# Output and down projections token-major, part of down in a 7-product block form, rope keys padded to full rows

## The chip, the cores and the metric

The kernel runs on one core of one Trainium2 chip. The metric is the time of the device in microseconds for one execution; the table below gives the runs and one execution taken with the hardware profiler. Engines are named as the profile names them: PE is TensorE's matmul, PEld its weight load, DVE is VectorE, ACT is ScalarE, POOL is GpSimd, SP issues DMAs.

## What is computed

One decoder layer for 256 tokens of width 2048, in fp32: three mixers side by side (a pool mixer, latent attention with 8 heads, attention to a memory of 256 tokens), an output projection with a residual, and a gated feed-forward of width 5632 with a short causal convolution, with a residual.

```python
h = rms_norm(x, g_mix[l])
z = h @ w_in[l]
z_pool, z_q, z_kv, z_kr, z_mq = jnp.split(z, IN_SPLITS, axis=-1)
...
x = x + jnp.concatenate([y_pool, y_mla, y_mem], axis=-1) @ w_o[l]
x = x + conv_glu_ffn(rms_norm(x, g_ffn[l]), w_gate[l], w_up[l], conv_w[l], conv_b[l], w_down[l])
...
return (jax.nn.silu(gc) * (h @ w_up)) @ w_down
...
k = jnp.concatenate([k_nope, k_r], axis=-1)
```

The third line from below closes the feed-forward; `gc` is the convolution of `h @ w_gate` along the tokens. The last line is from the latent attention: a head's key is 128 columns of its own and a rope key of 64 that all heads share.

## The kernel before

Every fp32 operand of a large product is split into a high part, rounded to the type that TensorE takes in one pass, and a low part, the rest. A product is then three: high x high, high x low, low x high. For weights `split_w` does it: ScalarE casts the high part (L90), VectorE subtracts it from the weights for the low part (L91), 1024 columns at a time. The parts lie in rings of three buffers (`wh`, `wl`), the raw weights in a ring of three buffers of 1 MB (`wr`), loaded through SP's queue by `load_w`.

There are two forms of product. `gemm_t` is feature-major: a weight tile of 128 x 128 is stationary, the activations of all 256 tokens move, with their high parts in columns 0 to 255 and their low parts in 256 to 511. The high weights take one matmul of 512 columns (L104), the low ones one of 256 (L107); the two halves of the result are added by VectorE. `gemm_n` is token-major: an activation tile (128 features x 128 tokens) is stationary and the weights move, 512 columns at a time, in three matmuls (L121 to L123) into one PSUM bank.

The order in time: keys and values of the memory (token-major), memory queries and rope key (token-major), latents and pool input (feature-major), queries and keys up (token-major), then for each of 8 heads `mla(h)` beside one `out_half(0, ...)` of the output projection, then the rest of the output projection (`out_half(1, ...)`), gate and up (44 feature tiles of 128), and down (16 output tiles, each over 44 tiles of the feed-forward). Instructions are placed by a scheduler, which moves a ready one ahead of one that waits; each engine then runs its own in the order in which they were placed.

In `mla` the scores of a head have a product over 128 rows (L577), one over the 64 rows of the rope part (L578), whose tiles hold two heads, one in rows 0 to 63 and one in 64 to 127, and a product in bf16 that adds the mask (L580); each fp32 product here is two instructions. The softmax follows; the probabilities are turned by TensorE, multiplied with the values, and split into `cat`.

The output projection adds into `xT`, which holds x feature-major. From it `h2`, the split input of the feed-forward, is made tile by tile, and the squares for the norm are summed over features (L603 to L616). The norm's factor `r1` is multiplied onto gate and up behind their products (L628). Down is feature-major, too; the result is added to `xT` (L655, L656) and leaves in 16 DMAs of 128 KB.

PSUM is two pools of four banks each: `psm` for the large products, `psa` for the others. `big` is one space of SBUF that holds the parts of the memory, then the queries, keys and values, then `h2`.

Of the kernel before, what the change touches and what calls it, by code (L numbers as in the profile page):

```python
# [18 lines left out]
P = 128  # L19
# [18 lines left out]
HS = 1024  # L38

# [11 lines left out]
# per-token tables: cos | sin (each NT x 32), rope gains of q | k (64 each), pool edge factors (4 x 16)  # L51
# [5 lines left out]
def layer(ctx, tc, xT_d, memT_d, vec_d, tab_d, w_z_d, w_mqkr_d, w_q_d, w_kv_d, w_mem_d, w_pool_d, w_o_d,  # L57
# [26 lines left out]
    def split_w(raw, o, n, cut=HS):  # L84
        """high and low parts of raw[:, o:o + n]"""
# [24 lines left out]
    def gemm_n(pss, hi, lo, act, k0, first, last):  # L110
        """pss[tt][j] (+)= act[:, k0:, tile tt].T @ W[:, :, span j]; tokens on partitions. hi/lo: [P, k, n]"""
# [13 lines left out]
    def split_act(dst, src, scale=None):  # L125
        """dst[:, :T], dst[:, T:] = high and low parts of src (times a per-partition scale)."""
# [16 lines left out]
    xT = const.tile([P, KD, T], F32, name="xT")  # L143
# [8 lines left out]
    # the tensor engine's clock is raised, and the activation tables are loaded, while the first loads are on their way  # L152
# [13 lines left out]
    mp = mix.enter_context(tc.tile_pool(name="mix", bufs=1))  # L166

# [14 lines left out]
    class SumSq:  # L182
        """sum over tiles and partitions of squares, per token"""
# [31 lines left out]
    def to_features(dst, src, tt, n, scale=None, eng=None):  # L215
        """dst[:, i, tile tt] = src[:, i * 128:].T (times a per-partition scale), i < n <= 4"""
# [116 lines left out]
    rsqrt_(rxb[:], ps[:, 0:T], 1.0 / D)  # L333

# [26 lines left out]
    def softmax_pv(ps, spans, f, v_of, dst):  # L361
        """ps: scores of each query tile at spans, keys in tiles of P; dst gets the parts of the output's transpose"""
# [12 lines left out]
        # turned: for each key tile, the query tiles that see it  # L375
# [25 lines left out]
    def half_add(dst, ps):  # L401
        """dst = ps[:, :T] + ps[:, T:]"""
# [23 lines left out]
    # scale of the normalised latents, per token: s = rx * (rx^2 mean(z^2) + eps)^-0.5  # L426
# [41 lines left out]
    qkv = big.tile([P, 32, T], F32, tag="act", name="qkv")  # L468
    qnT, knT, qrT, krT = qkv[:, 0:8], qkv[:, 8:16], qkv[:, 16:20], qkv[:, 20:24]
# [5 lines left out]
    def rotate(dst, src, s, tt, nh):  # L475
        """dst = rotated src [P, nh, 64] with the gained tables of side s"""
# [32 lines left out]
    # keys are scaled by f_k = ((s_kv^2 |kn|^2 + rx^2 |kr|^2) / QK + eps)^-0.5 and turned  # L509
# [43 lines left out]
    # f_q = s_q (s_q^2 mean + eps)^-0.5 / sqrt(QK), applied as the softmax scale  # L553
# [11 lines left out]
    for tt in range(NT):  # L565
# [3 lines left out]
        to_features(krT, t, tt, 4, None, "v")  # L569

# [1 line left out]
    def mla(h):  # L572
        ps = ps_aux()
        b = ROPE * (h % 2)
# [8 lines left out]
    def out_half(i, m):  # L583
        """x (+)= the part i of the output projection, for the pair of feature tiles m, m + 1"""
        raw = load_w(w_o_d[i][m // 2], STG)
        for j in range(2):
            ps = ps_main()
            if i == 0:
                gemm_t(ps, raw, j * HS, lambda k: cat[:, k, :] if k < 4 else catm[:, k - 4, :], range(8))
            else:  # L590
                gemm_t(ps, raw, j * HS, lambda k: cat[:, k, :], range(4, 12))
# [147 lines left out]
```

## Time and profile before

| | us |
|---|---|
| three runs, lowest, median, highest | 1044.50, 1044.92, 1044.95 |
| profiled execution, span from its first to its last instruction | 1043.6 |
| TensorE busy in it | 1034.8 |
| VectorE busy | 708.8 |
| ScalarE busy | 542.5 |

The span of the profiled execution leaves out what lies around it; it stands 1.3 us below the median of the runs. A matmul's record reaches from its start to a modelled end that lies past the start of the next, since matmuls are pipelined: the spacing of two starts is what one costs, and not the length of its record. The granted clock of TensorE is at full speed, 2.4 GHz, all through.

### The profile page before, as it was taken

The numbers are of one execution on the slowest core, as the hardware profiler recorded it, in microseconds if no ns is written. First come the engines' busy times: TensorE is split into PE (matmuls) and PEld (weight loads), VectorE is DVE, ScalarE is ACT, GpSimd is POOL, SyncE is SP. The second block draws the span as 40 slices with busy tenths as digits, with TensorE's granted clock in tenths as the row PEclk, the third lists the DMA queues.
The fourth block names the chain that finished last, engine by engine and source line by source line (L and its number), as shares of the span: only waits on it lengthen the run. The fifth ranks groups of instructions, "written<-read, shape, count | busy, mean of one in ns | idle before, by whom it ended". The sixth has DMA issues, their size and how long they took to land.

```text
span 1043.6 us, 14921 instructions
## 1 busy us (share of the span) xinstructions
PE 1034.8 (99%) x5852; PEld 897.2 (86%) x5852; DVE 708.8 (68%) x1141; ACT 542.5 (52%) x828; POOL 1.5 (0%) x10
## 2 busy tenths in 40 slices
PE   8999999999999999999999999999999999999998
PEld 6798888778888888888888888888888888888887
DVE  6967689766887777777777777777776554454453
ACT  7847666544666555555455455455454343333342
POOL 0000000000000000000000000000000000000000
PEclk9999999999999999999999999999999999999999
DMA  8555444333555555545555455555555665665661
GB/s 334 206 185 197 159 162 172 121 122 121 184 180 202 179 185 202 180 184 202 180 184 202 181 183 202 182 183 200 184 181 180 202 194 185 211 196 181 223 197 46
DMA packets 31030, 191.83 MB, mean 184 GB/s; under 512 B 3440, under 2 KB 6000, under 8 KB 10864
## 3 DMA queue, kind: packets, MB, share of 16 engines
q1 hardware_dynamic: 30672, 190.49, 52.7%
q8 instruction: 46, 0.75, 0.3%
q10 hardware_dynamic: 288, 0.38, 0.1%
q14 instruction: 24, 0.20, 0.0%
HBM read 188.77 MB, written 2.10 MB: 183 GB/s over the span
## 4 chain that ended last, share of the span: by engine, by line
PE 98%; DMA 1%; ACT 0%; DVE 0%; SPq 0%; issue 0%
PE psm L104 56%; PE psm L107 29%; PE psm L123 3%; PE psm L121 3%; PE psm L122 3%; PE psa L578 1%; PE psa L219 1%; DMA wr<-in_w_mem 1%; PE psa L385 1%; PE psa L577 1%; PE psa L380 1%; PE psa L393 0%; PE psa L386 0%; PE psa L580 0%; DVE wl L91 0%; ACT wh L90 0%
## 5 line engine op out<-in xcount | busy, mean ns | idle before, releaser
L91 DVE TENSOR_TENSOR wl<-wr,wh 128x1024 fp32r<-128x1024 f32 (+2 forms) x368 | 431.6, 1174 | 270.6 <-ACT wh L90 237.1
L90 ACT CAST wh<-wr 128x1024 fp32r<-128x1024 f32 (+2 forms) x368 | 371.2, 1009 | 438.3 <-PE psm L104 350.4
L104 PE MATMUL psm<-h,wh 128*128 128x512 f32 x1408 | 352.7, 392 | 0.0
L104 PEld LDWEIGHTS psm<-h,wh 128*128 128x128 f32 x1408 | 253.3, 189 | 45.5 <-DVE h L132 0.3
L107 PEld LDWEIGHTS psm<-h,wl 128*128 128x128 f32 x1408 | 192.1, 190 | 13.7
L107 PE MATMUL psm<-h,wl 128*128 128x256 f32 x1408 | 196.5, 282 | 0.0
L104 PE MATMUL psm<-aT,wh 128*128 128x512 f32 x704 | 177.9, 393 | 0.0
L104 PEld LDWEIGHTS psm<-aT,wh 128*128 128x128 f32 x704 | 125.9, 189 | 22.2
L107 PEld LDWEIGHTS psm<-aT,wl 128*128 128x128 f32 x704 | 97.0, 190 | 7.7
L107 PE MATMUL psm<-aT,wl 128*128 128x256 f32 x704 | 99.3, 282 | 0.0
L104 PE MATMUL psm<-cat,wh 128*128 128x512 f32 x192 | 52.0, 398 | 0.0
L642 DVE SCALAR_TENSOR_TENSOR gc<-g,vec,gc 128x255 f32<-128x255 f32 x88 | 42.2, 480 | 1.5
L104 PE MATMUL psm<-xg,wh 128*128 128x512 f32 x160 | 43.0, 401 | 0.0
L104 PEld LDWEIGHTS psm<-cat,wh 128*128 128x128 f32 x192 | 33.5, 189 | 4.9
L104 PEld LDWEIGHTS psm<-xg,wh 128*128 128x128 f32 x160 | 28.7, 189 | 4.9
L107 PEld LDWEIGHTS psm<-cat,wl 128*128 128x128 f32 x192 | 27.3, 190 | 2.6
L121 PE MATMUL psm<-wh,mg 128*128 128x512 f32 x64 | 25.1, 399 | 3.2 <-ACT mg L131 3.1
L107 PE MATMUL psm<-cat,wl 128*128 128x256 f32 x192 | 28.1, 282 | 0.0
L640 ACT ACTIVATE gc<-g,vec 128x256 f32<-128x256 f32 x44 | 26.3, 597 | 0.0
L123 PE MATMUL psm<-wl,mg 128*128 128x512 f32 x64 | 24.7, 396 | 0.9 <-DVE wl L91 0.9
L122 PE MATMUL psm<-wh,mg 128*128 128x512 f32 x64 | 25.3, 395 | 0.1
L107 PE MATMUL psm<-xg,wl 128*128 128x256 f32 x160 | 24.7, 289 | 0.0
(173 smaller groups left out, 840.0 us busy)
## 6 DMA issues: line engine op xcount, KB each, us to landing
wr<-in_w_g SPq DMA_DIRECT2D x44, 1024.0 KB, 4.9
wr<-in_w_u SPq DMA_DIRECT2D x44, 1024.0 KB, 4.8
wr<-in_w_dn SPq DMA_DIRECT2D x32, 1024.0 KB, 5.1
wr<-in_w_o SPq DMA_DIRECT2D x16, 1024.0 KB, 4.8
wr<-in_w_dn SPq DMA_DIRECT2D x16, 768.0 KB, 4.2
wr<-in_w_z SPq DMA_DIRECT2D x10, 1024.0 KB, 4.8
wr<-in_w_mqkr SPq DMA_DIRECT2D x8, 576.0 KB, 3.8
wr<-in_w_mem SPq DMA_DIRECT2D x4, 1024.0 KB, 7.2
```

The costliest lines, as they stand in the source:

```text
L90: nc.scalar.copy(hi[:, c:e], raw[:, o + c:o + e])
L91: nc.vector.tensor_tensor(lo[:, c:e], raw[:, o + c:o + e], hi[:, c:e].bitcast(F32), op=ALU.subtract)
L104: nc.tensor.matmul(ps[:, :2 * T], hi[:, i * P:(i + 1) * P], act(k), start=first and c + i == 0, stop=False, skip_group_check=True)
L107: nc.tensor.matmul(ps[:, T:2 * T], lo[:, i * P:(i + 1) * P], act(k)[:, 0:T], start=False, stop=end and i == len(kc) - 1, skip_group_check= ...
L121: nc.tensor.matmul(ps, xh, hi[:, i, o], start=first and i == 0, stop=False)
L122: nc.tensor.matmul(ps, xl, hi[:, i, o], start=False, stop=False)
L123: nc.tensor.matmul(ps, xh, lo[:, i, o], start=False, stop=last and i == nk - 1)
L219: nc.tensor.transpose(ps[:, i * P:(i + 1) * P], src[:, i * P:(i + 1) * P], identf[:])
L380: nc.tensor.transpose(tp[:, x * P:(x + 1) * P], p[:, a + k * P:a + (k + 1) * P], identf[:])
L385: nc.tensor.matmul(o[:, 0:T], v_of(0), pT[:, 0:T], start=True, stop=False, skip_group_check=True)
L640: nc.scalar.activation(gc[:], g[:], AF.Identity, bias=v("conv_b", f), scale=v("cw2", f))
L642: nc.vector.scalar_tensor_tensor(gc[:, d:T], g[:, 0:T - d], v(w, f), gc[:, d:T], op0=ALU.mult, op1=ALU.add)
```

## The change

The output projection becomes token-major. `out_part(i, n, pss, c)` takes half of the 8 row tiles of one part for 512 columns, with `gemm_n`; `out_add` adds two PSUM banks to `x1n`, which holds x token-major. It lies in the place of `xT` and is loaded from a new input `xn` by two DMAs of 1 MB on POOL's queue once the parts of x are made. The squares of x1 are summed by ScalarE while it squares (`out_done`), and x1 is also stored to a buffer in device memory, `x1s`, through POOL's queue. `turn(n)` turns four feature tiles of x1 with TensorE (8 transposes) and splits them into `h2`. The norm's factor is made per token (`rc`); for gate it is spread along the free dimension by a product of a diagonal matrix with ones (`r1`). Up is not multiplied by it any more: down's result is, per token, at its end. The last turned tiles and the norm come between the first and the second half of the first gate and up products.

Down becomes token-major, in two halves of 1024 columns (c). Its 44 row tiles are 22 pairs. For 13 of them (`plain`) a pair is 2 row tiles x 2 token tiles x 2 spans of 512 columns = 8 block products of three matmuls each. For the other 9 (2, 4, ... 18; `seven`) the 2 x 2 x 2 block product is done in 7 products. Their left factors are sums and differences of the blocks of the activations, made and split in `glu`. Their right factors are blocks of the weights and four differences of them, called F1 to F4 below (`F[:, 0]` to `F[:, 3]`), made by VectorE in `seven` (three instructions) in the place of `h2`, and split like weights: `b11` is one block, `b2` two, `t13` and `t24` two each. Three of the 7 products go into the banks of their own output block (`own`), four into common banks (`com`) that are combined into the four output blocks once per half (`common`). `finish` multiplies by `rc`, adds the residual that was read back from `x1s`, and stores 256 KB per block.

The rope keys of a head get a tile of their own, with the 64 rows of the other head zero, so that the rope product runs over 128 rows; the rope queries move to the place of the memory queries.

The core of the diff:

```diff
+NN = 512
...
+PAIRS = KF // 2
+SEVEN = tuple(range(2, 20, 2))
...
-    xT = const.tile([P, KD, T], F32, name="xT")
...
+    xT = mp.tile([P, KD, T], F32, tag="x", name="xT")
...
+    x1n = mp.tile([P, NT, D], F32, tag="x", name="x1n")
+    for tt in range(NT):
+        nc.gpsimd.dma_start(x1n[:, tt, :], xn_d[tt])
...
-    qnT, knT, qrT, krT = qkv[:, 0:8], qkv[:, 8:16], qkv[:, 16:20], qkv[:, 20:24]
+    qnT, knT, krT, qrT = qkv[:, 0:8], qkv[:, 8:16], qkv[:, 16:24], mqT
+    nc.gpsimd.memset(krT, 0.0)
...
-        to_features(krT, t, tt, 4, None, "v")
+        k4 = krT.rearrange("p (i e) t -> p i e t", e=2)
+        for e in range(2):
+            r = slice(e * ROPE, (e + 1) * ROPE)
+            nc.vector.tensor_copy(k4[r, :, e, tt * P:(tt + 1) * P], p3[r])
...
-            nc.tensor.matmul(ps[:, a:a + n], qrT[b:b + ROPE, h // 2, q], krT[b:b + ROPE, h // 2, 0:n],
-                             start=False, stop=False, skip_group_check=True)
+            nc.tensor.matmul(ps[:, a:a + n], qrT[:, h // 2, q], krT[:, h, 0:n], start=False, stop=False,
+                             skip_group_check=True)
...
+    def out_part(i, n, pss, c):
+        raw = load_w(w_o_d[i, n, c], STG)
+        for h in range(2):
+            hi, lo = split_w(raw, h * HS, HS)
+            w = [t[:].rearrange("p (k n) -> p k n", n=NN) for t in (hi, lo)]
+            k = c * 4 + h * 2
+            act, k = (cat, 4 + k) if i else (cat, k) if k < 4 else (catm, k - 4)
+            gemm_n(pss, *w, act, k, c + h == 0, c + h == 2)
+    def out_add(n, pss):
+        for tt in range(NT):
+            x = x1n[:, tt, n * NN:(n + 1) * NN]
+            nc.vector.tensor_tensor(x, x, pss[tt][0], op=ALU.add)
...
+        if h % 2 == 0:
+            pss = [[ps_main()[:]] for _ in range(NT)]
+        out_part(0, h // 2, pss, h % 2)
+        if h % 2 == 1:
+            out_add(h // 2, pss)
...
+    def out_done(n, pss):
+        out_add(n, pss)
+        for tt in range(NT):
+            x = x1n[:, tt, n * NN:(n + 1) * NN]
+            sq = tok()
+            nc.scalar.activation(sq[:], x, AF.Square, accum_out=ssx[:, tt, n:n + 1])
+            nc.gpsimd.dma_start(x1s[:, tt, n * NN:(n + 1) * NN], x)
+    def turn(n):
+        for m in range(4 * n, 4 * n + 4):
+            ps = ps_aux()
+            for tt in range(NT):
+                nc.tensor.transpose(ps[:, tt * P:(tt + 1) * P], x1n[:, tt, m * P:(m + 1) * P], identf[:])
+            split_act(h2[:, m, :], ps[:, 0:T], v("g_ffn", m))
+    for n in range(4):
+        pss = [[ps_main()[:]] for _ in range(NT)]
+        for c in range(2):
+            out_part(1, n, pss, c)
+        out_done(n, pss)
+        if n:
+            turn(n - 1)
...
+    def x1_rstd():
+        nc.vector.tensor_reduce(rc[:], ssx[:], axis=AX.X, op=ALU.add)
+        rsqrt_(rc[:], rc[:], 1.0 / D)
+        for tt in range(NT):
+            nc.vector.tensor_scalar(dg[:, tt * P:(tt + 1) * P], identf[:], rc[:, tt:tt + 1], None, op0=ALU.mult)
+        ps = ps_aux()
+        nc.tensor.matmul(ps[:, 0:T], ones[:], dg[:], start=True, stop=True)
+        nc.scalar.copy(r1[:], ps[:, 0:T])
...
-        nc.vector.tensor_tensor(t[:], t[:], r1[:], op=ALU.mult)
+        nc.vector.tensor_tensor(g[:], g[:], r1[:], op=ALU.mult)
...
+            hold[j] = fp.tile([P, 8, P], F32, tag="s8", name=nm("s8"), bufs=1)
+        s = hold[j]
+        o = 0 if e else 6
+        nc.vector.tensor_tensor(s[:, o:o + 2, :].rearrange("p a t -> p (a t)"), u[:], gc[:], op=ALU.mult)
+        if e:
+            for d, a, op, b in ((2, 7, ALU.add, 1), (3, 2, ALU.subtract, 6), (4, 6, ALU.subtract, 7),
+                                (5, 0, ALU.subtract, 3)):
+                nc.vector.tensor_tensor(s[:, d, :], s[:, a, :], s[:, b, :], op=op)
+            hi, lo = (aT[j][:, i].rearrange("p a t -> p (a t)") for i in range(2))
+            sf = s[:, 0:7, :].rearrange("p a t -> p (a t)")
+            nc.scalar.copy(hi, sf)
+            nc.vector.tensor_tensor(lo, sf, hi.bitcast(F32), op=ALU.subtract)
...
+    raws = [load_w(w[0], STG) for w in (w_g_d, w_u_d)]
+    pss = [ps_main() for _ in range(2)]
+    for ps, raw in zip(pss, raws):
+        gemm_t(ps, raw, 0, lambda k: h2[:, k, :], range(8), last=False)
+    turn(3)
+    x1_rstd()
+    mix.close()
+    fp = ctx.enter_context(tc.tile_pool(name="ffn", bufs=1))
+    for ps, raw in zip(pss, raws):
+        gemm_t(ps, raw, HS, lambda k: h2[:, k, :], range(8, KD), first=False)
+    glu(0, *pss)
...
+    dn = big.tile([P, 16, NN], F32, tag="act", name="dn")
...
+    def prod(ps, a, b, first, last):
+        nc.tensor.matmul(ps, a[0], b[0], start=first, stop=False)
+        nc.tensor.matmul(ps, a[1], b[0], start=False, stop=False)
+        nc.tensor.matmul(ps, a[0], b[1], start=False, stop=last)
+    def plain(c, j, own, first, last, by_bank=False):
+        raw = load_w(w_dn_d[c, j], STG)
+        ws = [split_w(raw, k * HS, HS) for k in range(2)]
+        order = [(k, t, n) for k in range(2) for t in range(NT) for n in range(2)]
+        if by_bank:
+            order.sort(key=lambda o: o[1:])
+        for k, t, n in order:
+            a = [aT[j][:, k, o + t * P:o + (t + 1) * P] for o in (0, T)]
+            s = n if k == 0 else 1 - n
+            prod(own[t, n], a, [w[:, s * NN:(s + 1) * NN] for w in ws[k]], first and k == 0, last and k == 1)
...
+    def seven(c, j, own, com, first, last):
+        raw = load_w(w_dn_d[c, j], STG)
+        r3 = raw[:].rearrange("p (b n) -> p b n", n=NN)
+        F = dn[:, 4 * (cnt[0] % 2):4 * (cnt[0] % 2) + 4, :]
+        cnt[0] += 1
+        nc.vector.tensor_tensor(F[:, 0:2], r3[:, 1:3], r3[:, 0:2], op=ALU.subtract)
+        b11 = split_w(raw, 0, NN)
+        b2 = split_w(raw, 2 * NN, HS)
+        nc.vector.tensor_tensor(F[:, 2], r3[:, 2], F[:, 0], op=ALU.subtract)
+        nc.vector.tensor_tensor(F[:, 3], r3[:, 3], F[:, 2], op=ALU.subtract)
+        Ff = F.rearrange("p b n -> p (b n)")
+        t13 = split_w(Ff, 0, HS)
+        t24 = split_w(Ff, HS, HS)
+        for (b, s), f, ps, own_ in (((b11, 0), 6, com[0], False), ((b2, 0), 5, own[0, 1], True),
+                                    ((b2, 1), 0, own[0, 0], True), ((t13, 0), 2, com[1], False),
+                                    ((t13, 1), 4, com[3], False), ((t24, 0), 3, com[2], False),
+                                    ((t24, 1), 1, own[1, 0], True)):
+            prod(ps, [aT[j][:, i, f, :] for i in range(2)], [w[:, s * NN:(s + 1) * NN] for w in b],
+                 first and not own_, last and not own_)
...
+        v1, u2, u3, u5 = (dn[:, 8 + i, :] for i in range(4))
...
+        elif step == 1:
+            nc.scalar.copy(v1, com[0])
+            nc.vector.tensor_tensor(u2, v1, com[2], op=ALU.add)
+            nc.vector.tensor_tensor(u3, u2, com[3], op=ALU.add)
+            nc.vector.tensor_tensor(u5, u3, com[1], op=ALU.add)
+            nc.vector.tensor_tensor(u2, u2, com[1], op=ALU.add)
+        else:
+            for i, u in enumerate((v1, u2, u3, u5)):
+                t = i // 2
+                nc.vector.scalar_tensor_tensor(dn[:, 12 + i, :], u, rc[:, t:t + 1], dn[:, 12 + i, :],
+                                               op0=ALU.mult, op1=ALU.add)
...
+    def finish(c, own, eng):
+        for t in range(NT):
+            for n in range(2):
+                o = dn[:, 12 + 2 * t + n, :]
+                nc.vector.scalar_tensor_tensor(o, own[t, n], rc[:, t:t + 1], o, op0=ALU.mult, op1=ALU.add)
+                eng.dma_start(out_d[t][:, c * HS + n * NN:c * HS + (n + 1) * NN], o)
...
+        own_ps, com_ps = (ps_main, ps_aux) if c else (ps_aux, ps_main)
+        own = {(t, n): own_ps()[:] for t in range(NT) for n in range(2)}
+        com = None
+        for j in range(PAIRS):
+            if j in SEVEN:
+                if com is None:
+                    com = [com_ps()[:] for _ in range(4)]
+                seven(c, j, own, com, j == SEVEN[0], j == SEVEN[-1])
+            else:
+                plain(c, j, own, j == 0, j == PAIRS - 1, by_bank=j == PAIRS - 1)
+            if j == 0 and done is not None:
+                finish(0, done, nc.gpsimd)
+            if j == PAIRS - 6:
+                common(c, None, 0)
+            if j == PAIRS - 3:
+                common(c, com, 1)
+            if j == PAIRS - 2:
+                common(c, com, 2)
+        done = own
+    finish(1, done, nc.sync)
...
+    w = a["w_down"][0].reshape(PAIRS, 2, P, 2, 2, NN)
+    w = np.stack([w[:, 0, :, :, 0], w[:, 0, :, :, 1], w[:, 1, :, :, 1], w[:, 1, :, :, 0]])
+    r["w_dn"] = w.transpose(3, 1, 2, 0, 4).reshape(2, PAIRS, P, STG)
```

## Rows read from the trace of the kernel before

**Rows 1.** The page's busy times: us, share of the span, instructions.

```profile
PE 1034.8 (99%) x5852; PEld 897.2 (86%) x5852; DVE 708.8 (68%) x1141; ACT 542.5 (52%) x828; POOL 1.5 (0%) x10
```

**Rows 2.** Stretches: range, length, busy us (instructions) by engine, PEclk, DMA share, GB/s.

```profile
56.00:83.00 27.00, 27.00 (x204) 26.80 (x202) 16.31 (x23) 13.69 (x24) 0.00 (x0) 1.00 0.65 218
...
187.00:257.00 70.00, 70.00 (x387) 54.24 (x387) 45.62 (x106) 32.80 (x66) 0.00 (x0) 1.00 0.34 117
...
307.00:798.00 491.00, 491.00 (x2815) 432.18 (x2815) 355.06 (x528) 260.64 (x399) 0.00 (x0) 1.00 0.54 188
...
798.00:1043.60 245.60, 242.10 (x1388) 212.54 (x1386) 116.98 (x126) 89.65 (x92) 0.00 (x0) 1.00 0.56 181
```

**Rows 3.** Chain that ended last, in time: start us, us, what.

```profile
500.83 1.84 PE psm L104 x8
...
668.43 1.84 PE psm L104 x8
...
855.62 1.86 PE psm L104 x8
...
870.99 1.86 PE psm L104 x8
```

**Rows 4.** Waits, 800 to 1040: total us, times, longest.

```profile
ACT wh L90 <- PE psm L104: 144.4, 91, 2.2
```

**Rows 5.** Timeline, PE, memory keys: start us, us, line, operation, out<-in.

```profile
22.51 0.39 PE L123 MATMUL psm<-wl,mg 128*128 128x512 f32 x1
...
36.79 0.39 PE L123 MATMUL psm<-wl,mg 128*128 128x512 f32 x1
```

**Rows 6.** Groups by line, 800 to 1040: count, busy us, mean ns, idle.

```profile
L91 DVE TENSOR_TENSOR wl<-wr,wh 128x1024 fp32r<-128x1024 f32 x76 | 93.0, 1224 | 94.4 <-ACT wh L90 94.4
...
L90 ACT CAST wh<-wr 128x1024 fp32r<-128x1024 f32 x75 | 78.7, 1049 | 116.4 <-PE psm L104 116.4
...
L91 DVE TENSOR_TENSOR wl<-wr,wh 128x512 fp32r<-128x512 f32 x16 | 11.1, 692 | 24.2 <-PE psm L107 24.2
...
L90 ACT CAST wh<-wr 128x512 fp32r<-128x512 f32 x16 | 9.9, 620 | 28.0 <-PE psm L104 28.0
```

**Rows 7.** Timeline, down: the last reader of a buffer, the next cast.

```profile
1030.16 2.00 PE L104 MATMUL psm<-aT,wh 128*128 128x512 f32 x8
...
1032.20 0.62 ACT L90 CAST wh<-wr 128x512 fp32r<-128x512 f32 x1 [1.75 <-PE psm L104]
```

**Rows 8.** Timeline, memory keys: four transposes and the product behind them.

```profile
52.37 0.60 PE L219 MATMUL psa<-identf,tok 128*128 128x128 f32 x4
...
52.72 0.48 PE L121 MATMUL psm<-wh,mg 128*128 128x512 f32 x1
```

**Rows 9.** Timeline, PE: the scores of one head.

```profile
196.12 0.39 PE L577 MATMUL psa<-qkv 128*128 128x128 f32 x2
...
196.92 0.65 PE L577 MATMUL psa<-qkv 128*128 128x256 f32 x2
...
198.13 0.23 PE L580 MATMUL psa<-cmask,identb 128*128 128x128 bf16 x1
...
198.17 0.71 PE L104 MATMUL psm<-catm,wh 128*128 128x512 f32 x2
```

**Rows 10.** Waits, whole span: total us, times, longest.

```profile
PEld psa L578 <- issue: 2.7, 8, 0.3
PEld L580 <- issue: 2.7, 8, 0.3
```

**Rows 11.** Timeline, PE: full-row products of 256 columns, two instructions each.

```profile
95.59 0.59 PE L385 MATMUL psa<-pT,mv 128*128 128x256 f32 x2
96.02 0.59 PE L386 MATMUL psa<-pT,mv 128*128 128x256 f32 x2
```

**Rows 12.** Timeline, PEld: first gate products, the last tile of h2.

```profile
306.57 0.19 PEld L104 LDWEIGHTS psm<-h,wh 128*128 128x128 f32 x1 [0.26 <-DVE h L132]
```

**Rows 13.** Timeline, the last output DMA.

```profile
1041.04 0.34 SPq L657 DMA_DIRECT2D out_t<-o  x1
```

More of the change, by code (lines that the diff above doesn't have):

```diff
@@ L613, in layer @@
-    ps = ps_aux()
-    nc.tensor.matmul(ps[:, 0:T], ones[:], acc[:], start=True, stop=True)
-    r1 = const.tile([P, T], F32, name="r1")
-    rsqrt_(r1[:], ps[:, 0:T], 1.0 / D)
-    mix.close()
-    fp = ctx.enter_context(tc.tile_pool(name="ffn", bufs=1))
-    aT = fp.tile([P, KF, 2 * T], F32R, name="aT")
-    def scaled(ps, tag):
-        t = fp.tile([P, T], F32, tag=tag, name=nm(tag), bufs=2)
+        if h % 2 == 0:
+            pss = [[ps_main()[:]] for _ in range(NT)]
+        out_part(0, h // 2, pss, h % 2)
@@ new lines, in turn @@
+    def turn(n):
[11 more added lines that the diff above has]
+            turn(n - 1)
+    rc = const.tile([P, NT], F32, name="rc")
@@ L626, in scaled, with halves, glu @@
+    aT = {}
+    hold = {}
+    def halves(ps, tag):
+        t = fp.tile([P, T], F32, tag=tag, name=nm(tag), bufs=1)
         nc.scalar.copy(t[:], ps[:, 0:T])
         nc.vector.tensor_tensor(t[:], t[:], ps[:, T:2 * T], op=ALU.add)
-        nc.vector.tensor_tensor(t[:], t[:], r1[:], op=ALU.mult)
         return t
-    for f in range(KF):
-        raw = load_w(w_g_d[f], STG)
-        psg = ps_main()
-        gemm_t(psg, raw, 0, lambda k: h2[:, k, :], range(KD))
-        raw = load_w(w_u_d[f], STG)
-        psu = ps_main()
-        gemm_t(psu, raw, 0, lambda k: h2[:, k, :], range(KD))
-        g = scaled(psg, "g")
-        gc = fp.tile([P, T], F32, tag="gc", name=nm("gc"), bufs=2)
+    def glu(f, psg, psu):
+        g = halves(psg, "g")
+        nc.vector.tensor_tensor(g[:], g[:], r1[:], op=ALU.mult)
+        gc = fp.tile([P, T], F32, tag="gc", name=nm("gc"), bufs=1)
@@ L643, in layer @@
         nc.scalar.activation(gc[:], gc[:], AF.Silu)
-        u = scaled(psu, "u")
-        nc.vector.tensor_tensor(u[:], u[:], gc[:], op=ALU.mult)
-        split_act(aT[:, f, :], u[:])
-    for m in range(KD):
-        ps = ps_main()
-        for k in range(0, KF, STG // P):
-            n = min(STG // P, KF - k)
-            raw = load_w(w_dn_d[m][:, k * P:(k + n) * P], n * P)
-            gemm_t(ps, raw, 0, lambda i: aT[:, i, :], range(k, k + n), first=k == 0, last=k + n == KF)
-        o = fp.tile([P, T], F32, tag="o", name=nm("o"), bufs=2)
-        nc.vector.tensor_tensor(o[:], xT[:, m, :], ps[:, 0:T], op=ALU.add)
-        nc.vector.tensor_tensor(o[:], o[:], ps[:, T:2 * T], op=ALU.add)
-        nc.sync.dma_start(out_d[m], o[:])
+        u = halves(psu, "u")
@@ new lines, in glu @@
+        j, e = f // 2, f % 2
+        if j not in SEVEN:
+            if e == 0:
+                aT[j] = fp.tile([P, 2, 2 * T], F32R, name=nm("aT"))
+            nc.vector.tensor_tensor(u[:], u[:], gc[:], op=ALU.mult)
+            split_act(aT[j][:, e, :], u[:])
+            return
+        if e == 0:
+            aT[j] = fp.tile([P, 2, 7, P], F32R, name=nm("aS"))
+            hold[j] = fp.tile([P, 8, P], F32, tag="s8", name=nm("s8"), bufs=1)
+        s = hold[j]
+        o = 0 if e else 6
+        nc.vector.tensor_tensor(s[:, o:o + 2, :].rearrange("p a t -> p (a t)"), u[:], gc[:], op=ALU.mult)
@@ new lines, in layer @@
+    raws = [load_w(w[0], STG) for w in (w_g_d, w_u_d)]
[9 more added lines that the diff above has]
+    glu(0, *pss)
+    for f in range(1, KF):
+        pss = []
+        for w in (w_g_d, w_u_d):
+            raw = load_w(w[f], STG)
+            pss.append(ps_main())
+            gemm_t(pss[-1], raw, 0, lambda k: h2[:, k, :], range(KD))
+        glu(f, *pss)
@@ L732 @@
         args.append(nc.dram_tensor(f"in_{name}", x.shape, F32, kind="ExternalInput").ap())
-    args.append(nc.dram_tensor("out_t", (KD, P, T), F32, kind="ExternalOutput").ap())
+    args.append(nc.dram_tensor("out_t", (NT, P, D), F32, kind="ExternalOutput").ap())
     with _tile.TileContext(nc) as tc:
```

52 lines of the change are left out of this document (22 added, 30 removed).

## Prediction

> **What bounds the kernel now.** Read the busy times first: TensorE is busy for 99% of the span [rows 1]. A busy TensorE may still wait inside, so read the table by stretches next: from 56 us on it is full in every stretch shown but for the tail of the last, and VectorE is busy for only 117 of the last 245.6 us, the down projection [rows 2]. Then read the chain of work that ended last, in order of time: in gate and up 60 groups of eight wide products lie between 500.83 and 668.43, 2.793 us each, and one output tile of down follows the other after 15.37 us [rows 3]. 15.37 us is 5.5 times 2.79 us, so neither stage has a gap: time is the number of matmuls times their spacing. Last, the waits of the down stage: ScalarE's casts wait for TensorE to free their buffers, 144.4 us in total [rows 4]. The splitting engines are ahead, held by the ring of three `wh` and three `wl`. So the change pays what it takes off TensorE, as long as VectorE stays ahead in its new place.
>
> **The spacing.** One feature-major group (8 matmuls of 512 columns, 8 of 256; 6144 columns) costs 2.793 us [rows 3]. The token-major form that both projections change to already runs in the memory keys and values: between two matmuls of L123 lie 63 matmuls of 512 columns, 14.28 us, 0.2267 us each, with the same pattern of stationary activations and moving weights [rows 5].
>
> **Down.** Before: 16 output tiles x 44 row tiles = 88 groups x 2.793 = 245.8 us. After, for each half of the columns: 13 plain pairs x 24 + 9 pairs x 21 matmuls = 501, together 1002 x 0.2267 = 227.2 us. Gain 18.6 us: 54 matmuls fewer are 12.2, the wide form 6.4. TensorE gets this only if VectorE keeps up, so I lay one seven pair and the plain pair behind it side by side. Prices [rows 6]: cast 1.05 us for 1024 columns, 0.62 for 512; subtraction 1.22 and 0.69. The differences F have no row of their own; they are subtractions of the same shapes and I take those. VectorE per seven pair: F1 and F2 together 1.22, F3 and F4 0.69 each, low parts 0.69 + 3 x 1.22, sum 6.95 us, against 21 x 0.227 = 4.76 us of TensorE. Alone, this would make VectorE the bound. The plain pair has 2 x 1.22 = 2.45 against 24 x 0.227 = 5.44. Both: 9.40 of VectorE in 10.20 of TensorE. The ring decides whether that closes. Let a seven pair start on TensorE at 0. `b11` and `b2` sit in the ring already. `t13` needs the buffers of the plain half that TensorE has just left; the cast starts 0.04 us after the record of the last reader [rows 7], which at 0.39 runs 0.17 past its slot [rows 5]. So: cast 0.2 to 1.25, subtraction 1.29 to 2.51. TensorE wants that low part after 9 + 2 matmuls, at 2.49: it waits about 0.1. `t24` (cast to 2.30, subtraction 2.51 to 3.74) is wanted at about 3.95. The plain halves are subtracted to 4.96 and 6.19, wanted at 5.3 and 8.0. Then VectorE makes the next pair's F and low parts of `b11` and `b2`, in whatever order, until 11.4, when the next seven pair has been running for 1.1; it could not take `t13` before 1.29 in any case. So the cycle closes with 0.1 us lost per seven pair: 18 x 0.1 = +1.8 us. Below this it can be 0; above, each further 0.1 us in those handovers costs another 1.8. The combinations of `common` and `finish` fall where five plain pairs follow each other (19 to 21, then 0 and 1), with 3 us of VectorE to spare in each: nothing. Loads: 1 MB per 5.1 us, 206 GB/s; the trace carried 218 GB/s beside a full TensorE [rows 2]: nothing.
>
> **Output projection.** 32 groups x 2.793 = 89.4 us before; 16 row tiles x 24 = 384 x 0.2267 = 87.1 after: gain 2.3. VectorE has fewer operations there (16 additions of 512 for 64 of 256).
>
> **Transposes added.** x1 is now token-major and is turned for the feed-forward: 32 transposes. Four of them lie between 52.37 and 52.72 us, where the next product starts [rows 8]: 0.088 each, +2.8 us. The record of one lasts four times as long. The Trainium skill (TensorE: Matmul & The Clock Gate, Part 4: PE-mode transpose) gives about 275 ns for one within a kernel; by that the term would be 8.8 us and the sum 6.0 higher. The rows agree with the page on duration and not on spacing.
>
> **Rope keys.** A score now has 128 rows instead of 64 in its rope product, at the same columns. In one head, the first query tile takes 0.80 us and the second 1.25 (196.12, 196.92, 198.17) [rows 9]. In each head a 64-row weight load, and the mask's load behind it, wait 0.33 us for nothing that the profile names [rows 10]. Full-row products of 256 columns are 0.43 us apart per two instructions [rows 11]; with 0.07 for the mask that makes 0.50 and 0.93. Saved 0.30 + 0.32 per head, 5.0 us in eight; TensorE is full there [rows 2]. Ends: 2.7 if only one of the two kinds of wait goes, 5.4 if both go whole. I take 5.0, by full-row products of the same kind. The Trainium skill (the same page, Part 3, The mechanism) states that a weight load runs under a matmul only where its row group differs; by that the padding would gain nothing. The waits of [rows 10] show the opposite: the load for other rows is the one that waits. The memset of the keys (POOL) and the second copy per token tile (VectorE, 0.69 [rows 6]) lie before attention, beside products that wait for neither.
>
> **Seams.** (a) The first gate product needs the last four turned tiles. Addition (0.69), eight transposes (0.7), then four casts and subtractions mixed with weight splits end about 6 us after the last output product; the first halves of gate and up, the transposes and four wide products give 5.6 + 0.7 + 0.9 = 7.2 us of cover. Without cover up to 3 us. The trace of before loses 0.26 us there [rows 12]; I take +0.5. The matmul of the norm waits on a chain of similar length. (b) `xn`, 2 MB through POOL's queue, beside loads that already move 218 GB/s [rows 2]: nothing waits for x1n for 100 us, but weights may be late by up to 2 us; +0.3. The stores of x1 also go through POOL's queue; only the feed-forward's buffers wait for them, 8 us later. (c) The last output DMA is issued 2.6 us before the end of the span [rows 13]; it doubles to 256 KB and three others run ahead of it: 0 to +1, I take +0.3. Gate and up keep 88 x 5.59 us; VectorE loses a multiplication per tile there and gains four short ones per seven pair, with 355 of 491 us busy [rows 2]: nothing.
>
> **Sum.** -18.6 - 2.3 - 5.0 + 2.8 + 1.8 + 0.5 + 0.3 + 0.3 = -20.2 us against the profiled span of 1043.6, so a span of 1023.4. The median of the runs, 1044.92, is 1.3 above that span: forecast 1024.7 us.
>
> **Rivals.**
> - *Handovers dearer than worked out.* A seven pair loses 0.5 us rather than 0.1, since `t13` has no slack at all: +7.2, 1032 (1029 to 1040). For it: three engines hand over in a row. Against: [rows 7], 0.04 us per handover.
> - *VectorE becomes the bound: slower.* If its order makes it wait for casts of F within the seven pair instead of working ahead in the plain pair, each seven pair costs TensorE VectorE's 6.95 us, not 4.86: 18 x 2.09 = 37.6, 1062 us. It decides from 1.2 us lost per seven pair, where the whole gain of 20.2 is used up. Against: the 0.8 us to spare per two pairs, and that F needs no ring buffer.
> - *The form does not do what it says:* token-major columns cost what the old ones do, 2.793 / 12 = 0.233 per matmul: +6.1 in down, +2.3 in the output projection, 1033. Against: 63 spacings [rows 5].
> - *The start of the feed-forward waits* for turned tiles or the norm: +3 to +8, 1028 to 1033.
> - *The page's transpose price* holds in these runs of eight: +6.0, 1031.
> - *The page's load rule* holds: no gain from padding, +5.0, 1030.
>
> **How the numbers follow.** Forecast 61% (1021 to 1029), dearer handovers 17, slower 7, form 4, seam 6, transpose price 3, load rule 2. The lower end takes rope at 5.4, no handover loss and no seams: 1021.6, rounded down by one for spacing: 1020.5. The upper, 1035, takes in the forecast, the seam, the form, the page's two and most of the dearer handovers; 17 to 20 in 100 lie outside. 0.2% is 2.1 us, about what a measurement of this kernel can tell from no change: faster 0.91 (all but the slower rival and the far end of the handovers), same 0.02, slower 0.07.
>
> **What would show it.** Down: first to last product 229 us; VectorE busy for some 206 of them (18 x 6.95 + 26 x 2.45, and 17 for `common` and `finish`); between a `b11` and the next, 10.3 us per two pairs. TensorE waiting for `wl` in seven pairs by over 0.5 us is the first rival, over 1.2 the second. Rope: no waits of the loads in the scores, 8.1 us per head instead of 8.85 (less 0.62 and 0.15). Turned tiles: eight transposes in 0.7 us. A gap of over 1 us at the first gate product would show the seam. If VectorE's F rows are well above 1.22 and 0.69, the prediction is wrong where it is thinnest.

## The result

The changed kernel takes 1033.22 us (1032.49 to 1033.57), the one before 1044.93 on the same chip: a ratio of 0.9883, 95% interval 0.9869 to 0.9897. It is faster by 11.7 us. The time lies within the forecast range, on the right side of no change, but only 58% of the 20.2 us that I had worked out were there.

The profiled execution of after has a span of 1031.5 us. Its busy times [rows 1]:

```profile
PE 1018.7 (99%) x5350; PEld 867.6 (84%) x5350; DVE 760.4 (74%) x1140; ACT 572.6 (56%) x850; POOL 11.1 (1%) x25
```

TensorE has 502 matmuls fewer and is busy for 16.1 us less, while the span is only 12.1 us shorter: more of it than before is waiting. The table by stretches says where; first the score phase, then down from its first to its last product (columns as in [rows 2]):

```profile
187.00:257.00 70.00, 69.98 (x341) 55.19 (x341) 43.22 (x85) 33.96 (x66) 0.00 (x0) 1.00 0.34 123
...
791.00:1027.00 236.00, 230.95 (x1004) 187.87 (x1003) 192.20 (x202) 119.87 (x127) 2.16 (x4) 0.99 0.56 198
```

In down TensorE stands still for 5 us, and its granted clock is not quite full. Cut at the first score, the first gate product, the first product of down and the end of its last (its start and one spacing), the two traces compare as follows. The forecast's terms are those of its sum, sorted into the stages where they fall (24 of the 32 transposes lie ahead of the first gate product; `xn` is loaded at 50 us).

| stretch | before, us | after, us | difference | forecast |
|---|---|---|---|---|
| start to first score | 186.84 | 185.88 | -1.0 | +0.3 |
| first score to first gate product | 114.87 | 111.95 | -2.9 | -5.2 |
| gate and up | 492.26 | 493.27 | +1.0 | +1.2 |
| down | 246.08 | 236.21 | -9.9 | -16.8 |
| behind the last product | 3.59 | 4.16 | +0.6 | +0.3 |

The first line shows no effect of the change: the loads at the very start land earlier or later from run to run, and the versions of the changed kernel below, whose edits lie behind this stretch, began their scores between 185.2 and 187.0. Two gaps are left to explain: 6.9 us in down, and 2.3 around attention and the output projection.

The chain of work that ended last shows the first gap at once. Before, down's part of it is matmuls alone [rows 3] but for the last additions and the output. After, three weight loads stand in it (start us, us, what):

```profile
912.06 7.91 DMA wr<-in_w_dn
957.99 6.93 DMA wr<-in_w_dn
990.96 4.97 DMA wr<-in_w_dn
```

The third of them cost TensorE only 0.3 us, and the load behind a wait at 845 that cost more isn't in this chain. The waits between 791 and 1028 (total us, times, longest) [rows 4] have rows that before has none of:

```profile
DVE dn L760 <- DMA wr<-in_w_dn: 13.4, 10, 2.9
ACT wh L94 <- DVE wl L95: 9.0, 5, 2.1
PEld psa L742 <- DVE wl L95: 5.9, 4, 2.7
PE psa L742 <- DVE wl L95: 4.2, 2, 2.2
...
PEld psm L742 <- DVE wl L95: 2.5, 5, 1.2
...
PE psm L742 <- DVE wl L95: 0.8, 1, 0.8
```

L760 is the instruction that makes F1 and F2; it waits ten times for its weights. L742 is the third matmul of a product, the one that needs a low part; it waits for VectorE's L95, which makes low parts. VectorE's timeline at the worst place joins the two (start us, us, engine, line, operation; in brackets the idle time before and what ended it):

```profile
919.99 1.22 DVE L760 TENSOR_TENSOR dn<-wr 128x1024 f32<-128x1024 f32 x1 [2.90 <-DMA wr<-in_w_dn]
921.13 2.35 DVE L95 TENSOR_TENSOR wl<-dn,wh 128x1024 fp32r<-128x1024 f32 x2
```

The second line makes the low parts of `t13` and `t24` of the seven pair that TensorE is working on. The first makes the F of the *next* seven pair, whose weights have not landed. F had two buffers, so nothing kept the scheduler from placing the next F early; VectorE runs in order, so the current low parts wait behind it, 2.90 us for the load and 1.22 for the subtraction. TensorE started no matmul between 919.79 and 922.40.

The same trace separates two things that might each be to blame. In 12 of the 18 seven pairs the next F stands ahead of the current `t13`, in 11 of them directly. Ten of the 12 wait for the load, by 0.50 to 2.90 us; two (801.54, with the subtraction for F3 behind it, and 931.36) don't wait. Four of the 12:

```profile
845.02 1.23 DVE L760 TENSOR_TENSOR dn<-wr 128x1024 f32<-128x1024 f32 x1 [2.11 <-DMA wr<-in_w_dn]
...
865.11 1.23 DVE L760 TENSOR_TENSOR dn<-wr 128x1024 f32<-128x1024 f32 x1 [0.58 <-DMA wr<-in_w_dn]
...
931.36 1.22 DVE L760 TENSOR_TENSOR dn<-wr 128x1024 f32<-128x1024 f32 x1
...
964.94 1.22 DVE L760 TENSOR_TENSOR dn<-wr 128x1024 f32<-128x1024 f32 x1 [2.78 <-DMA wr<-in_w_dn]
```

TensorE's spacing was stretched by 0.92 us behind the first of these, by less than 0.1 behind the second, by nothing behind the third and by 2.16 behind the last. Behind 801.54 it was 0.3 us. So the order alone, or with a wait of up to 1.0 us, costs 0.3 us at most; order and a wait of over 2 us together cost more. That happened three times (845, 920, 965). With the stretched spacings that followed they make 7.4 of the 9.1 us by which down's spacings exceed 0.2267 us. Seven of the ten loads took 4.7 to 5.0 us, as most do; the other three, 5.9 us (issued at 839), 7.9 (912) and 6.9 (958), are those of these three waits.

### The profile page after: what moved, and what is told of

The parts are those of the page before. It is cut to its first block, busy times and chain, and to the rows that moved or that the text cites. A ratio compares the mean times of both kernels' runs of the same rounds, so it can differ in the third digit from the quotient of the medians.

```text
span 1031.5 us, 14051 instructions
## 1 busy us (share of the span) xinstructions
PE 1018.7 (99%) x5350; PEld 867.6 (84%) x5350; DVE 760.4 (74%) x1140; ACT 572.6 (56%) x850; POOL 11.1 (1%) x25
## 4 chain that ended last, share of the span: by engine, by line
PE 95%; DMA 2%; DVE 1%; issue 1%; ACT 0%; DVEq 0%
PE psm L108 35%; PE psm L111 18%; PE psm L127 6%; PE psm L125 6%; PE psm L126 6%; PE psa L742 4%; PE psa L741 3%; PE psa L740 3%; PE psm L742 3%; PE psm L741 3%; PE psm L740 3%; DMA wr<-in_w_dn 2%; DVE wl L95 1%; PE psa L223 1%; PE psa L392 1%
## 5 line engine op out<-in xcount | busy, mean ns | idle before, releaser
L95 DVE TENSOR_TENSOR wl<-wr,wh 128x1024 fp32r<-128x1024 f32 (+2 forms) x360 | 418.0, 1170 | 194.9 <-ACT wh L94 192.6
L111 PEld LDWEIGHTS psm<-h,wl 128*128 128x128 f32 x1408 | 192.1, 190 | 13.7
L94 ACT CAST wh<-dn 128x1024 fp32r<-128x1024 f32 x36 | 36.1, 1052 | 30.1 <-PE psm L741 15.1
L95 DVE TENSOR_TENSOR wl<-dn,wh 128x1024 fp32r<-128x1024 f32 x36 | 42.4, 1220 | 9.3 <-ACT wh L94 9.3
L742 PE MATMUL psa<-wl,aT 128*128 128x512 f32 x104 | 40.6, 390 | 0.0
L741 PE MATMUL psm<-wh,aT 128*128 128x512 f32 x104 | 40.5, 390 | 0.0
L740 PE MATMUL psm<-wh,aT 128*128 128x512 f32 x104 | 40.5, 389 | 0.0
L740 PE MATMUL psa<-wh,aT 128*128 128x512 f32 x104 | 40.5, 389 | 0.0
L741 PE MATMUL psa<-wh,aT 128*128 128x512 f32 x104 | 40.5, 389 | 0.0
L742 PE MATMUL psm<-wl,aT 128*128 128x512 f32 x104 | 40.4, 390 | 0.0
L125 PE MATMUL psm<-wh,cat 128*128 128x512 f32 x96 | 38.5, 401 | 0.0
L127 PE MATMUL psm<-wl,cat 128*128 128x512 f32 x96 | 37.8, 394 | 0.0
L126 PE MATMUL psm<-wh,cat 128*128 128x512 f32 x96 | 37.6, 392 | 0.0
L760 DVE TENSOR_TENSOR dn<-wr 128x1024 f32<-128x1024 f32 x18 | 22.0, 1222 | 13.9 <-DMA wr<-in_w_dn 13.4
L742 PE MATMUL psa<-wl,aS 128*128 128x512 f32 x63 | 25.3, 407 | 4.3 <-DVE wl L95 4.2
```

The source lines that it names most:

```text
L94: nc.scalar.copy(hi[:, c:e], raw[:, o + c:o + e])
L95: nc.vector.tensor_tensor(lo[:, c:e], raw[:, o + c:o + e], hi[:, c:e].bitcast(F32), op=ALU.subtract)
L111: nc.tensor.matmul(ps[:, T:2 * T], lo[:, i * P:(i + 1) * P], act(k)[:, 0:T], start=False, stop=end and i == len(kc) - 1, skip_group_check= ...
L125: nc.tensor.matmul(ps, xh, hi[:, i, o], start=first and i == 0, stop=False)
L126: nc.tensor.matmul(ps, xl, hi[:, i, o], start=False, stop=False)
L127: nc.tensor.matmul(ps, xh, lo[:, i, o], start=False, stop=last and i == nk - 1)
```

## The experiments

Theory A: the scheduler's order on VectorE, F ahead of the current low parts, turns a late load into a wait of TensorE. Theory B: VectorE is simply too full in the seven pairs, my rival of the prediction. Within A it was open what makes the loads late; the residual reads (L782) are issued by SP among them. Unless said otherwise an edit is to the kernel after. The times of before beside these runs were 1045.15 to 1045.34 us.

**Reads of the residual on another queue (e1_reads).**

```
-                    nc.sync.dma_start(dn[:, 12 + 2 * t + n, :], x1s[:, t, o:o + NN])
+                    nc.gpsimd.dma_start(dn[:, 12 + 2 * t + n, :], x1s[:, t, o:o + NN])
```

> The changed kernel with the eight reads of the stored x1 moved from SP's queue to POOL's. Theory A (queue order): in the second half of the columns these reads stand on SP ahead of weight loads and wait there for the output DMAs of the first half; the loads behind them land up to 8 us after their issue, and TensorE waits 2.4 us and then runs some 2 us at the low clock. Without them on SP that stretch is free: 4.4 us less than the changed kernel, 1028.8 us. Theory B (VectorE is the bound of down): nothing changes, 1033.2 within 0.7.

Measured: 1032.93 us (1032.61 to 1036.03), ratio 0.9893 [0.9878, 0.9908]. No gain; A's number was wrong here. The two loads issued at 908 and 912 still took 7.6 and 7.5 us, where most take 4.8, and the wait at 919 is 2.45 us, 2.90 without the edit:

```profile
919.29 1.22 DVE L760 TENSOR_TENSOR dn<-wr 128x1024 f32<-128x1024 f32 x1 [2.45 <-DMA wr<-in_w_dn]
```

So SP's order was not what made these loads late. At that time 1 MB of output and 1 MB of residual move beside them (four DMAs of 256 KB each). Which of the two slows the loads wasn't separated; in the trace of after, the loads issued at 789.9 and 796.2, beside four such reads alone, took 4.7 and 4.8 us.

**One buffer for F (e2_f_one).** The write of the next F1 and F2 must then wait until the low part of `t13` has read the current ones. VectorE's work is the same, only its order is forced.

```
-        F = dn[:, 4 * (cnt[0] % 2):4 * (cnt[0] % 2) + 4, :]
+        F = dn[:, 0:4, :]
```

> The changed kernel with one buffer for the differences F instead of two, so that the first differences of a seven pair can't be made before the last parts of the seven pair before are split. Theory A: with two buffers they stand on VectorE ahead of the low part of t13 that TensorE waits for, and hold it up when their load is late; behind it they hold up nothing. The waits near 804, 846, 966 and 998 us go, 3.6 us: 1029.6. Theory B: VectorE has less freedom and the same work; 1033.2 or more.

Measured: 1025.72 us (1024.94 to 1025.9), ratio 0.9813 [0.9799, 0.9826]: 7.5 us faster than the change, with one buffer less, and better than A had asked: its 3.6 us left out the wait at 920, which it had put down to the reads. In the trace no F stands ahead of a current `t13`, and L760 waits for no load at all (same groups by line as [rows 6], 792 to 1020; the 0.5 us belong to the first one):

```profile
L760 DVE TENSOR_TENSOR dn<-wr 128x1024 f32<-128x1024 f32 x18 | 21.9, 1217 | 0.5 <-PE psm L111 0.5
```

The loads did not become punctual: two, issued at 907.7 and 911.3, took 8.3 us, but VectorE comes to the F that needs them only after they have landed. TensorE is full in down, to be compared with the row for 791 to 1027 above:

```profile
791.80:1019.80 228.00, 228.00 (x1004) 186.62 (x1003) 190.95 (x202) 119.68 (x127) 2.17 (x4) 1.00 0.58 205
```

Down took 227.95 us; 1002 x 0.2267 is 227.2.

**Both edits (e3_both).**

> Both edits: reads on POOL's queue and one buffer for F. Theory A: no wait of TensorE over 0.3 us in down, first to last product 228 to 230 us, 8 us less than the changed kernel: 1025.2. Theory B: 1033.2 or more.

Measured: 1025.83 us, ratio 0.9815 [0.9802, 0.9829], the same as with one buffer alone. With the order forced, the queue of the reads makes no difference here.

**The first subtraction on GpSimd (e8_pool).** Two F buffers; only L760 moves, so that the wait for the load stands on an engine with no low parts queued behind it (GpSimd also issues the four output DMAs of the first half).

```
-        nc.vector.tensor_tensor(F[:, 0:2], r3[:, 1:3], r3[:, 0:2], op=ALU.subtract)
+        nc.gpsimd.tensor_tensor(F[:, 0:2], r3[:, 1:3], r3[:, 0:2], op=ALU.subtract)
```

> The changed kernel with its two F buffers kept, and only the first, 1024-column subtraction of each seven pair moved from VectorE to GpSimd. If the loss comes from VectorE standing in front of a weight load with other pairs' low parts queued behind it, the wait for the load moves to GpSimd, where nothing else of down is queued, and the time comes near 1026 (to 1029, if GpSimd is much slower than 1.22 us at this operation). If the loss comes from the late loads themselves, or from holding two F buffers, it stays at 1033.

Measured: 1059.68 us, ratio 1.0137 [1.0121, 1.0152]. Neither was right; the run does not test A, because it brings a cost of its own. The subtraction takes 2.39 us on GpSimd, and VectorE's low part beside it takes 3.28 us in place of 1.21. GpSimd's line, and then the groups on VectorE's L95 from 862 to 870 (ns, min/median/max):

```profile
864.30 2.39 POOL L760 TENSOR_TENSOR dn<-wr 128x1024 f32<-128x1024 f32 x1 [7.16 <-DMA wr<-in_w_dn]
```

```profile
L95 DVE TENSOR_TENSOR wl<-dn,wh x2: 1212/2244/3276, 864.5 to 867.7; 128x1024 fp32r<-128x1024 f32 x2
```

The subtraction on VectorE began at 864.50 and ended at 867.77, about 1.1 us after GpSimd's had ended, as if it had done its work only then. The Trainium skill (SBUF — State Buffer, "SBUF: two separate sides") states just that: a VectorE instruction with two inputs in SBUF and a GpSimd instruction that reads SBUF share a pair of ports, and the later of them waits for the whole of the other. The trace agrees. Here it was `t13`'s low part that was hit, the very one that TensorE needs next; the mean of the 36 low parts of F rose to 1.78 us from 1.22, and TensorE waited for low parts in most of the seven pairs.

**The seven pairs take the weights of the plain pair before (e11_raw).**

```
-        raw = load_w(w_dn_d[c, j], STG)
+        raw = seen[0]
```

(in `seven`; `plain` keeps its buffer in `seen[0]`.)

> The changed kernel with its two F buffers and its order kept as far as the planner keeps it, but a seven pair takes the weights that the plain pair before it has loaded (so it leaves out the loads of 18 of 44 pairs of down, and its output isn't the reference's). F's first subtraction then has nothing to wait for. If the loss comes from a late load in front of which VectorE stands still, there is no such wait left, the low parts are delayed by at most the 1.2 us of the subtraction itself, and the time comes near 1026. If the mere place of that subtraction, ahead of the low part that TensorE wants next, makes the loss, it stays above 1030.  A third case: the planner, with the weights at hand, moves F further ahead and the loss is moved, not removed; then the waits of TensorE for low parts stay at a dozen or more.

Measured: 1025.18 us (1024.34 to 1025.75), ratio 0.9808 [0.9793, 0.9822]. The time is A's, but the run proves less than it should: with the weights at hand the scheduler put the next F 5 us or more ahead of the current `t13` and no longer directly ahead of it (807.53 and 812.60, say), and VectorE stands idle for some 1.3 us before `t13`'s low part. So place and lateness changed together. One wait of TensorE of 1.0 us is left, at 907, for a plain pair's low part behind additions of `finish` and the next F. (The expectation calls the scheduler the planner.) What separates them is the list of L760 in the section above, and that one F buffer removes the loss with loads as late as ever.

**VectorE's slack (e10_one, e10_three).** To the version with one F buffer, the last subtraction of F repeated once, or three times, with the same result.

```
         nc.vector.tensor_tensor(F[:, 3], r3[:, 3], F[:, 2], op=ALU.subtract)
+        nc.vector.tensor_tensor(F[:, 3], r3[:, 3], F[:, 2], op=ALU.subtract)
```

> The version with one F buffer (1025.7 us) and the 512-column subtraction behind F's last block issued twice, so 0.69 us more of VectorE in each of 18 seven pairs, 12.4 us in all. VectorE stood idle for 33 us in down in that version, most of it waiting for ScalarE's rounded copies. If VectorE isn't the bound of down, the time stays within 1 us of 1025.7. If it is (the rival that I had named), the time goes up by 8 to 12 us, to 1034 to 1038.

> The version with one F buffer and the last 512-column subtraction issued four times in place of once: 18 x 3 x 0.69 = 37 us more of VectorE in down. With one extra the time stayed (1024.5) and 23 us of VectorE's idle time before low parts were left, where 25 more are now asked for. If that idle time is all usable, the time goes up by 1 to 4 us; if TensorE pays for each extra in the seven pair itself (the rival that I had named, VectorE's seven-pair share not worked off beside the plain pair), by 20 to 25.

Measured: 1024.46 us with one (ratio 0.9803 [0.9789, 0.9818]) and 1039.91 with three (0.9950 [0.9934, 0.9967]). The first is free (in the traces down's products span 227.8 us with it, 227.7 without), so B falls: VectorE does not bound the change. But three cost 14 us, between the two times expected: more than by the idle time left, less than if each extra were paid in full. The F of one seven pair and the next now lie 11.05 us apart:

```profile
837.96 1.22 DVE L760 TENSOR_TENSOR dn<-wr 128x1024 f32<-128x1024 f32 x1
...
849.01 1.22 DVE L760 TENSOR_TENSOR dn<-wr 128x1024 f32<-128x1024 f32 x1
```

There VectorE sets the pace, and most of TensorE's waits stand at the first matmul with `t24` (L740, the first matmul of a product; it needs a cast, which waits for VectorE's last repeated subtraction):

```profile
PEld psa L740 <- ACT wh L94: 8.5, 14, 1.5
PEld psm L740 <- ACT wh L94: 8.2, 14, 1.2
```

11.05 less the three extras (2.07) is 8.98 us of VectorE per two pairs, against 10.20 of TensorE: by this estimate a slack of 1.2 us. One extra of 0.69 fits, three exceed it by 0.85, and 16 such cycles make 13.6 us; down grew by 13.7. My 9.40 was the sum of records, which overlap by nearly 0.1 us where VectorE's instructions follow each other.

**No seven-product pairs (e5_no_seven).**

```
-SEVEN = tuple(range(2, 20, 2))
+SEVEN = ()
```

> The changed kernel with no seven-product pair at all: 44 plain pairs of 24 wide matmuls, 1056 in place of 1002, and none of the differences F; the wide form, the padded keys and the token-major output projection stay. The order theory (waits of VectorE for a late weight load in front of the current seven pair's low parts eat half of the form's gain) expects no wait in down, so 1056 by 0.2267 us = 239.4 us from the first to the last matmul of down, against 236.2 in the changed kernel: about 3.3 us more, 1036.5 us; and about 11 us above the version with one F buffer (1025.7). The rival that the wide matmuls of down themselves run slower than 0.2267 us expects more than 1040.

Measured: 1036.12 us (1035.95 to 1036.25), ratio 0.9914 [0.9899, 0.9928]; 1036.5 was expected. Down lasted 239.4 us, 1056 x 0.2267 to the tenth, with VectorE busy for 111 of 239 us. So the wide form alone gives what its spacing says. The seven products are worth 10.4 us with one F buffer, and 2.9 as the change has them.

**Rope keys padded, alone, in the kernel before (e6_rope).**

```
-    qnT, knT, qrT, krT = qkv[:, 0:8], qkv[:, 8:16], qkv[:, 16:20], qkv[:, 20:24]
+    qnT, knT, krT, qrT = qkv[:, 0:8], qkv[:, 8:16], qkv[:, 16:24], mqT
...
-            nc.tensor.matmul(ps[:, a:a + n], qrT[b:b + ROPE, h // 2, q], krT[b:b + ROPE, h // 2, 0:n],
+            nc.tensor.matmul(ps[:, a:a + n], qrT[:, h // 2, q], krT[:, h, 0:n], start=False, stop=False,
```

> The kernel before with the padded rope keys alone. By the prediction's rows 5.0 us less than before, 1039.9; by the sum over the scores in the trace of the changed kernel 4.5 less, 1040.4. If a load of other rows is not what costs (the rival rule), no change: 1044.9.

Measured: 1041.75 us (1040.54 to 1042.04), ratio 0.9966 [0.9953, 0.9978]: -3.4 us, less than either number expected. In its trace the stretch from the first score to the first gate product is 4.2 us shorter than before; the first score came 0.4 us later, a difference of the size by which the starts vary.

**Ten seven pairs of 22 (e7_ten).** One F buffer, the seven pairs at 1, 3, ... 19; two scratch tensors shared to make room, and the reads on GpSimd's queue.

```
-SEVEN = tuple(range(2, 20, 2))
+SEVEN = tuple(range(1, 20, 2))
```

> A version meant to be faster than both: one F buffer, ten seven-product pairs of 22 in each half (every odd pair from 1 to 19) in place of nine, residual reads issued by GpSimd, and two scratch tensors shared with others. Two pairs less by 3 wide matmuls of 0.2267 us each is 1.4 us less than 1025.7, so about 1024.4, if the order of down holds; the rival (the combinations behind the tenth pair come up against the last plain pairs, or the shared scratch of the gate holds the FFN up) expects 1026 or more.

Measured: 1025.29 us (1025.13 to 1025.51), ratio 0.9810 [0.9794, 0.9827]. The difference to nine pairs cannot be told from none. Down itself is 1.3 us shorter (226.6 us against 227.95), as 6 matmuls fewer ask; the rest of its time did not follow. The version to keep is the change with one F buffer.

## Why the prediction was right or wrong

**The number.** The time lies in the range of 1020.5 to 1035, but above the 1021 to 1029 that were given 61 in 100. It came there by a mechanism that is none of the rivals; that the room left for them held it was luck.

**Down, -16.8 forecast, -9.9 measured.** The step that failed is the sentence that VectorE makes the next pair's F "in whatever order". I had laid out the seven pair by engine times and asked only whether the work fits; it does, as the run with one extra subtraction shows. The amounts were right, too: VectorE's records in down add up to 204.7 us, 206 forecast, and L760 took the 1.22 us that I had assumed. I had not asked what VectorE's next instruction waits for. Two buffers let the scheduler put an instruction that waits for a transfer ahead of one that TensorE needs at once. With the order forced, down gains 18.1 us, a little more than the 16.8 forecast: then the handovers for which I had put 1.8 us cost little: all 1002 spacings together exceed 0.2267 us by 0.8 us. The whole kernel, at 1025.72, then lies 1.0 us above the 1024.7 forecast.

The sentence on loads ("nothing") failed with it. It compared a mean rate, 206 against 218 GB/s, and down after moves 198. But a rate says nothing of when one load lands: most took 4.7 to 4.9 us, those beside outputs and residuals up to 8.0, and single ones elsewhere 5.9 and 6.9 (issued at 839 and 958), for which I found no reason. That the combinations of `common` and `finish` cost nothing held for VectorE and not for their transfers, which met the loads.

**The rivals.** Dearer handovers, 1032, had the right size and the wrong mechanism: the long waits of TensorE for `wl` lie in three places, not in each seven pair. VectorE as the bound fell (e10_one); what it looks like when it is the bound, e10_three shows. "The form does no cheaper" fell by e5_no_seven. The seam to the feed-forward cost no more than the forecast: gate and up grew by 1.0 us, 0.8 of it eight transposes.

**Rope keys, -5.0 forecast.** 4.2 us in the trace with padding alone. The loads' waits [rows 10] are gone, and one head's scores now take 1.45 us in place of 2.05 [rows 9], 0.60 against 0.62 forecast:

```profile
197.43 0.39 PE L592 MATMUL psa<-qkv 128*128 128x128 f32 x2
197.65 0.39 PE L593 MATMUL psa<-qkv,mqT 128*128 128x128 f32 x2
...
197.93 0.65 PE L592 MATMUL psa<-qkv 128*128 128x256 f32 x2
198.42 0.59 PE L593 MATMUL psa<-qkv,mqT 128*128 128x256 f32 x2
...
198.88 0.48 PE L126 MATMUL psm<-wh,catm 128*128 128x512 f32 x1
```

Eight of these are 4.8 us; about half a microsecond is given back in the products between them. By the rule of the Trainium skill that the prediction cites (TensorE: Matmul & The Clock Gate, Part 3, The mechanism), that a weight load runs under a matmul only where its row group differs, padding would have gained nothing; the run with padding alone contradicts it.

**Transposes, +2.8 forecast.** The eight just ahead of the first gate product, and the products behind them:

```profile
297.04 1.03 PE L640 MATMUL psa<-identf,x1n 128*128 128x128 f32 x8
297.83 1.39 PE L108 MATMUL psm<-h,wh 128*128 128x512 f32 x5
```

0.79 us for eight, 0.099 each (0.088 by [rows 8]): +3.2 in all. At the 275 ns that the prediction cites from the Trainium skill (the same page, Part 4: PE-mode transpose) it would have been 2.2 us. A record here lasts 0.27 us, so the trace agrees with that figure on the duration of one; the spacing is about a third of it (the prediction has a quarter).

**Output projection, -2.3 forecast.** About -1.1: the stretch that e6_rope leaves at 110.67 us is 111.95 after, +1.28, of which the 24 transposes are 2.37. Where it runs undisturbed it has the forecast spacing (nine spacings, 2.04 us):

```profile
294.77 0.39 PE L127 MATMUL psm<-wl,cat 128*128 128x512 f32 x1
...
296.81 0.39 PE L127 MATMUL psm<-wl,cat 128*128 128x512 f32 x1
```

Beside attention some 35 of its spacings are near 0.32 us, most of them where it resumes behind another product, as at 195.29 to 195.61. The term priced the undisturbed form for a phase that is interrupted all the time. How much of that is a loss and how much is only the way that spacings split at an interruption, I did not settle.

**Tail, +0.3 forecast,** +0.6 measured.

Two sums of the working are off by little and bear on nothing above: by its own terms VectorE's cycle ends at 10.7 us, not 11.4, and the lower end comes to 1021.4, not 1021.6.

## What to carry to other kernels

Whether an engine has time for added work is half of the question; the other half is what each of its instructions waits for, and what stands behind it. A second buffer is also a permission for the scheduler: where it lets an instruction that waits for a transfer go ahead of one that the bounding engine needs next, taking the buffer away can be the faster choice, as it was here by 7.5 us. Look for the added instruction in the list of waits, and price a load by its latest landing, not by its mean rate.

## What was not expected of the hardware

TensorE's clock. After it had started nothing from 919.79 to 922.40, its matmuls were 0.43 us apart until 925.5, about twice the usual 0.2267, the lower of its two levels (1.2 GHz). The granted clock by stretches of 10 us:

```profile
910.00:920.00 10.00, 10.00 (x45) 8.08 (x44) 4.56 (x7) 4.54 (x6) 0.00 (x0) 1.00 0.94 323
920.00:930.00 10.00, 7.77 (x27) 6.19 (x27) 7.84 (x8) 3.12 (x4) 0.00 (x0) 0.83 0.52 183
...
960.00:970.00 10.00, 8.00 (x35) 6.24 (x34) 7.19 (x8) 5.38 (x6) 0.00 (x0) 1.00 0.51 194
```

That cost another 1.7 us. A wait only a little shorter, from 964.97 to 967.36, left the clock at 1.00. In e8_pool, a wait of 4.8 us at 934.52 was followed by 0.79 from 940 to 950, but a wait from 865.66 to 867.83, the shortest of these, was also followed by 0.52 from 869.0 to 872.4. So the length of the last wait alone doesn't tell whether the clock falls; what else decides it, no run here was made to show.

The other is the pair of VectorE and GpSimd: an instruction of 1.21 us took 3.28 beside one of 2.39 on GpSimd.
